# Last norm of a diffusion backbone: most of the mean summed ahead, the gain vector multiplied in earlier, the scaling divided anew

## The chip, the cores and the metric

The kernel runs on one core of one Trainium2 chip. The metric is the device time of one execution in microseconds (us), the median of several runs; lower is better. A core has five engines that run at the same time and wait for each other by semaphores: TensorE (PE, matmuls; PEld is its weight load), VectorE (DVE), ScalarE (ACT), GpSimd (POOL) and SyncE (SP, which only issues DMAs here). ACT and POOL issue DMAs too.

## What is computed

One layer of a backbone for 256 latent and 256 context tokens of width 2048, then a last RMSNorm with its own gain vector. Cut to the end, which the change touches:

```python
def rms_norm(x, g):
    y = x * rsqrt(mean(x * x, axis=-1) + 1e-6)
    return y * g

x = x + gt_a * o_l
h = rms_norm(x, g_ffn) * (1.0 + sc_f) + sh_f
x = x + gt_f * ((silu(h @ wg) * (h @ wu)) @ wd)     # wd: 5632 x 2048
return rms_norm(x, g_final)                         # (1, 256, 2048), float32
```

All of it is float32. Each matmul is made of three with split operands (a high and a low part in the fp32r type).

## The kernel before, in words

Tokens lie on the 128 partitions, in two halves t = 0 and t = 1. Weights are streamed from memory in pieces of 128 x 512 (256 KB); ACT writes the high part (`whi`, L142), DVE the low part (`wlo`, L145), and PE does the three matmuls of each pair (L165, L166, L168). The order of instructions on each engine is the order in which the program writes them down.

The last product (`ffn_wd`) runs in three groups of rows; the last group makes the output columns final. Its blocks of 512 columns are `nb` = 0 to 3. For `nb` 0 to 2, `down_evac` adds the block into the residual `x2` (L1135, L1136), squares it on ACT with a running sum per token into one column of `ss3` (L1137), and multiplies `x2` in place by the gain vector `g_final` (`gfin`, L1139). The in-place multiply must come behind the square, which reads the same columns.

Block `nb` = 3 is done by itself, t = 0 first with 512 columns, then t = 1 in two halves of 256 columns, so that what follows the very last matmul is short (L1156 to L1180). After the matmuls of a part: gate multiply (L1165), residual add (L1166), square with its sum (L1167, which writes its squares over the gate product `yv`). After the last part of a t: the sums in `ss3` are added up (L1169), scaled by 1/2048 with the epsilon added (`rstd_of`, L175), raised to the power -1/2 on POOL (L177). Then the scaling by this factor `r`: block 3 on DVE with the gain vector in the same instruction (L1172), block 0 on DVE (L1176), blocks 1 and 2 on ACT (L1178). Each block then goes to memory with a DMA of 256 KB (L1180): blocks 3 and 1 from SP, blocks 0 and 2 from ACT, in the order 3, 0, 1, 2.

Buffers come from pools that lie one behind the other in SBUF, in the order in which they are opened, one row from the left and one from the right; a name of a pool has as many buffers as the pool says, and each takes a multiple of 32 bytes of a partition. The pool `small` (six buffers for each name) is opened early on the left; behind it come a small pad, the identity, and the streaming pool with `raw`, `whi` and `wlo`, whose first buffer starts at byte 20480 of its partition, then all other pools of the left side (among them `res` with `x2`, `gate` and `tm`, and `ff`). The `y` blocks that the last stores read are in a pool of the right side.

Of the kernel before, what the change touches and what calls it, by code (L numbers as in the profile page):

```python
# [10 lines left out]
F32 = mybir.dt.float32  # L11
F32R = mybir.dt.float32r
AF = mybir.ActivationFunctionType
ALU = mybir.AluOpType
AX = mybir.AxisListType
PSUM = bass.MemoryType.PSUM

P = 128
D = 2048
# [4 lines left out]
EPS = 1e-6  # L24
# [63 lines left out]
def hybrid_dit_kernel(ctx: ExitStack, tc: tile.TileContext, a, out):  # L88
    nc = tc.nc
    pe, act, dve, pool, sp = nc.tensor, nc.scalar, nc.vector, nc.gpsimd, nc.sync  # L90
# [4 lines left out]
    ss3 = const.tile([P, 2, 8], F32, name="ss3")  # L95
    small = ctx.enter_context(tc.tile_pool(name="small", bufs=6))
# [23 lines left out]
    def acc():  # L120
        return psA.tile([P, 512], F32, name="acc")
# [48 lines left out]
    def sub(pair, *sl):  # L170
        return pair[0][sl], pair[1][sl]

    def rstd_of(ssum, n, elems):
        v = small.tile([P, 8], F32, name="ms")
        dve.tensor_scalar(out=v[:, :n], in0=ssum, scalar1=1.0 / elems, scalar2=EPS, op0=ALU.mult, op1=ALU.add)  # L175
        r = small.tile([P, 8], F32, name="rstd")
        pool.tensor_tensor(out=r[:, :n], in0=v[:, :n], in1=mhalf[:, :n], op=ALU.pow)  # L177
        return r

    def tsl(t):  # L180
        return slice(t * P, (t + 1) * P)
# [44 lines left out]
    mhalf = const.tile([P, 8], F32, name="mhalf")  # L226
# [708 lines left out]
    res = ctx.enter_context(tc.tile_pool(name="res", bufs=1))  # L935
    x2 = res.tile([P, 2, D], F32, name="x2")
# [113 lines left out]
    y = [opool.tile([P, 2, 512], F32, name="y", tag="o", bufs=4) for _ in range(4)]  # L1050

    def gu(w, fb):
        accs = [acc() for _ in range(2)]
        for k2 in range(0, KC, 2):
            w_ = stream_w(w, k2, fb * 512, 512)
            mm3s([j for t in range(2) for j in gu_jobs(accs[t], w_, k2, t)])
            side.pump(2.6)
        return accs

    def act_T(sg, ps, pair, t, blocks):  # L1060
        dve.tensor_tensor(out=sg, in0=ps, in1=sg, op=ALU.mult)
        if blocks:


            tr = res.tile([P, 512], F32, name="tm", bufs=2)
            for b in range(4):
                dve.transpose(tr[:, tsl(b)].rearrange("p (j n) -> p j n", j=4), sg.rearrange("p (j b n) -> p b j n", j=4, b=4)[:, b])
            yield 0.0, 1.0
            td = dram.tile([P, 512], F32, name="sgd", bufs=4)
            pool.dma_start(td, tr)  # L1070
            tT = ff.tile([P, 4, 4, 32], F32, name="sg_T", bufs=2)
            dv = td.rearrange("(a p) (b r) -> b p a r", a=4, b=4)
            for b in range(4):
                pool.dma_start(tT[32 * b:32 * b + 32].rearrange("p a j n -> p a (j n)"), dv[b])
            yield 0.0, 14.0
            v = tT.rearrange("p a j n -> p j a n")
            hi, lo = [x[:, :, tsl(t)].rearrange("p j (a n) -> p j a n", a=4) for x in pair]
            act.copy(hi, v)
            dve.tensor_tensor(out=lo, in0=v, in1=hi.bitcast(F32), op=ALU.subtract)
            yield 0.0, 0.0  # L1080
            return
        yield 0.0, 1.5
        transposes_ff(pair, sg, t)
        yield 0.43, 0.0
# [11 lines left out]
    def gate_raw(src, shape):  # L1096
        raw = ff.tile(shape, F32, name="graw", bufs=4)
        pool.dma_start(raw, src)
        return raw

    gate_f = add_ada(5, 6.0, gate_raw, ahead=3)
    for gi, (f0, f1) in enumerate(groups):
        last = gi == len(groups) - 1
        aT, tasks = {}, {}
        for fb in range(f0, f1):
            ga = gu(a["ffn_wg"], fb) if fb else first_g
            sg = []
            for t in range(2):
                s_ = ff.tile([P, 512], F32, name="sg", bufs=4)
                act.activation(s_, ga[t], AF.Silu)  # L1110
                sg.append(s_)
            ua = gu(a["ffn_wu"], fb)
            aT[fb] = (ff.tile([P, 4, S], F32R, name="ah", bufs=6), ff.tile([P, 4, S], F32R, name="al", bufs=6))
            tasks[fb] = [side.add(act_T(sg[t], ua[t], aT[fb], t, fb < f1 - 1), lane="e", width=4) for t in range(2)]
        if gi == 1:
            side.finish(*gate_f)
            gtf = gate_rows(5, res)
            gf = [gate_raw(a["g_final"][i * 1024:(i + 1) * 1024].partition_broadcast(P), [P, 1024]) for i in range(2)]

            def gfin(c):  # L1120
                return gf[c.start // 1024][:, c.start % 1024:c.start % 1024 + c.stop - c.start]

        def down_jobs(ps, w_, fb, j, t):
            return [(ps, sub(aT[fb], slice(None), jj, tsl(t)), w_[jj - j], fb == f0 and jj == 0, fb == f1 - 1 and jj == 3) for jj in (j, j + 1)]

        def down_evac(ps, nb, t):
            c = slice(nb * 512, (nb + 1) * 512)
            if gi == 0:
                act.copy(y[nb][:, t, :], ps)
            elif not last:  # L1130
                dve.tensor_tensor(out=y[nb][:, t, :], in0=ps, in1=y[nb][:, t, :], op=ALU.add)
                dve.tensor_tensor(out=y[nb][:, t, :], in0=y[nb][:, t, :], in1=gtf[:, c], op=ALU.mult)
                dve.tensor_tensor(out=x2[:, t, c], in0=x2[:, t, c], in1=y[nb][:, t, :], op=ALU.add)
            else:
                dve.tensor_tensor(out=y[nb][:, t, :], in0=ps, in1=gtf[:, c], op=ALU.mult)  # L1135
                dve.tensor_tensor(out=x2[:, t, c], in0=x2[:, t, c], in1=y[nb][:, t, :], op=ALU.add)  # L1136
                act.activation(y[nb][:, t, :], x2[:, t, c], AF.Square, accum_out=ss3[:, t, nb:nb + 1])  # L1137
                if nb < 3:
                    dve.tensor_tensor(out=x2[:, t, c], in0=x2[:, t, c], in1=gfin(c), op=ALU.mult)  # L1139

        for nb in range(4 - last):
            accs = [acc() for _ in range(2)]
            for fb in range(f0, f1):
                side.finish(*tasks[fb])
                for j in (0, 2):
                    w_ = stream_w(a["ffn_wd"], fb * 4 + j, nb * 512, 512)
                    mm3s([q for t in range(2) for q in down_jobs(accs[t], w_, fb, j, t)])
                    side.pump(2.6)
            for t in range(2):
                down_evac(accs[t], nb, t)  # L1150
# [5 lines left out]
    for t in range(2):  # L1156
        for c0, cn in (((0, 512),) if t == 0 else ((0, 256), (256, 256))):
            ps = acc()
            for n, (fb, j) in enumerate(steps):
                if t == 0:  # L1160
                    w_keep[fb, j] = stream_w(a["ffn_wd"], fb * 4 + j, 3 * 512, 512, (rt2, 8) if n < 4 else None)
                mm3s([(ps[:, :cn], sub(aT[fb], slice(None), j + kk, tsl(t)), sub(w_keep[fb, j][kk], slice(None), slice(c0, c0 + cn)), n == 0 and kk == 0, n == len(steps) - 1 and kk == 1) for kk in range(2)])
            c = slice(3 * 512 + c0, 3 * 512 + c0 + cn)
            yv = y[3][:, t, c0:c0 + cn]
            dve.tensor_tensor(out=yv, in0=ps[:, :cn], in1=gtf[:, c], op=ALU.mult)  # L1165
            dve.tensor_tensor(out=x2[:, t, c], in0=x2[:, t, c], in1=yv, op=ALU.add)  # L1166
            act.activation(yv, x2[:, t, c], AF.Square, accum_out=ss3[:, t, 3 + (c0 > 0):4 + (c0 > 0)])  # L1167
        ss = small.tile([P, 8], F32, name="ss")
        dve.tensor_reduce(out=ss[:, 0:1], in_=ss3[:, t, :4 + t], axis=AX.X, op=ALU.add)  # L1169
        r = rstd_of(ss[:, 0:1], 1, D)  # L1170
        c = slice(3 * 512, D)
        dve.scalar_tensor_tensor(out=y[3][:, t, :], in0=x2[:, t, c], scalar=r[:, 0:1], in1=gfin(c), op0=ALU.mult, op1=ALU.mult)  # L1172
        for nb in range(3):
            c = slice(nb * 512, (nb + 1) * 512)
            if nb == 0:
                dve.tensor_scalar(out=y[nb][:, t, :], in0=x2[:, t, c], scalar1=r[:, 0:1], scalar2=None, op0=ALU.mult)  # L1176
            else:
                act.activation(y[nb][:, t, :], x2[:, t, c], AF.Copy, scale=r[:, 0:1])  # L1178
        for nb in (3, 0, 1, 2):
            (sp if nb % 2 else act).dma_start(out[tsl(t), nb * 512:(nb + 1) * 512], y[nb][:, t, :])  # L1180
    po.close()


# [59 lines left out]
```

## Time and profile before

| | us |
|---|---|
| median of 3 runs (lowest, highest) | 1357.15 (1356.35, 1359.22) |
| the profiled execution | 1355.29 |
| its span, first to last instruction | 1353.5 |
| PE busy in the span | 1324.0 (98%) |
| DVE busy | 923.2 (68%) |
| ACT busy | 625.7 (46%) |

The profile shows one execution. Start times count from the span's start. A row of the chain of waits gives start, duration and what was running; a row of the timeline gives start, duration, engine, line, operation, output and inputs, and in brackets how long the engine had been idle and what it had waited for. A row of windows gives for a stretch the busy time of each engine with its instructions, the TensorE clock as a share of full speed, the mean busy share of the 16 DMA engines and the rate that they moved. A row of groups gives line, engine, operation, shapes, count, then busy time and the mean nanoseconds of one, then idle time before them.

### The profile page before, as it was taken

To read this page: it belongs to the slowest core of one execution; us is meant where nothing else is said; L and a number is where in the kernel's file an instruction comes from. 1 tells how busy PE (TensorE), PEld (TensorE's weight loads), DVE (VectorE), ACT (ScalarE), POOL (GpSimd) and SP (SyncE) were. 2 spreads that over 40 slices of the span, in tenths; PEclk is the share of its full clock that TensorE was granted. 3 is DMA by queue.
4 is the path that set the end of the run, shared out by engine and by line. 5 is a ranking of instruction groups with operands and counts; after the bars stand their busy time and mean duration, and the time that the engine had idled before them with its cause. 6 is when DMAs were issued, how large, how long until landed. Compare 5 with 4: busy or idle time off the path is not lost.

```text
span 1353.5 us, 21027 instructions
## 1 busy us (share of the span) xinstructions
PE 1324.0 (98%) x7018; PEld 1077.5 (80%) x7018; DVE 923.2 (68%) x1687; ACT 625.7 (46%) x1183; POOL 99.6 (7%) x159
## 2 busy tenths in 40 slices
PE   6999999999999999999999999999999999999997
PEld 4788888778886777777888888888888888888886
DVE  4577789998679747778887954445555566556565
ACT  4532343564334435557445444444444444444453
POOL 1110000100000000000322200001001000011000
PEclk9999999999999999999999999999999999999999
DMA  9999996586687756455999855567667655676553
GB/s 367 344 356 323 322 364 220 171 268 213 198 262 262 247 166 212 135 184 164 344 368 340 307 191 192 193 196 219 210 212 228 218 193 185 203 226 224 193 178 129
DMA packets 190161, 322.29 MB, mean 238 GB/s; under 512 B 22466, under 2 KB 62436, under 8 KB 189028
## 3 DMA queue, kind: packets, MB, share of 16 engines
q1 hardware_dynamic: 177568, 285.28, 63.8%
q0 software_dynamic: 9136, 32.53, 6.5%
q10 hardware_dynamic: 3348, 3.13, 0.7%
q8 instruction: 55, 0.90, 0.3%
q14 instruction: 54, 0.44, 0.1%
HBM read 314.56 MB, written 6.31 MB: 237 GB/s over the span
## 4 chain that ended last, share of the span: by engine, by line
PE 68%; DVE 1%; ACT 1%; DMA 0%; issue 0%; POOL 0%; POOLq 0%; DVEq 0%; SPq 0%; ACTq 0%
PE acc L165 21%; PE acc L168 21%; PE acc L166 21%; PE m L862 1%; PE m L607 1%; PE m L861 1%; PE m L913 1%; PE m L897 1%; PE m L658 1%; DVE wlo L145 0%; PE m L165 0%; PE m L166 0%; PE m L168 0%; ACT whi L142 0%; DMA raw<-in_w_out_dram 0%; PE m L385 0%
## 5 line engine op out<-in xcount | busy, mean ns | idle before, releaser
L145 DVE TENSOR_TENSOR wlo<-raw,whi 128x512 fp32r<-128x512 f32 (+1 forms) x764 | 490.4, 680 | 286.0 <-ACT whi L142 281.5
L142 ACT CAST whi<-raw 128x512 fp32r<-128x512 f32 (+1 forms) x764 | 437.6, 615 | 520.2 <-PE acc L166 427.5
L165 PE MATMUL acc<-whi,h_hi 128*128 128x512 f32 x704 | 274.2, 390 | 0.7 <-ACT h_hi L1013 0.7
L166 PE MATMUL acc<-whi,h_lo 128*128 128x512 f32 x704 | 274.1, 389 | 0.4 <-DVE h_lo L1014 0.4
L168 PE MATMUL acc<-wlo,h_hi 128*128 128x512 f32 x704 | 190.8, 390 | 0.0
L165 PE MATMUL acc<-whi,h 128*128 128x512 f32 (+1 forms) x416 | 161.6, 392 | 1.2 <-ACT tok L791 0.5
L166 PE MATMUL acc<-whi,h 128*128 128x512 f32 (+1 forms) x416 | 157.1, 379 | 0.0
L168 PEld LDWEIGHTS acc<-wlo,h_hi 128*128 128x128 f32 x704 | 132.1, 188 | 28.5 <-DVE wlo L145 1.2
L165 PEld LDWEIGHTS acc<-whi,h_hi 128*128 128x128 f32 x704 | 132.2, 188 | 28.2 <-ACT h_hi L1013 1.1
L166 PEld LDWEIGHTS acc<-whi,h_lo 128*128 128x128 f32 x704 | 132.2, 188 | 28.0 <-DVE h_lo L1014 0.7
L165 PE MATMUL acc<-whi,ah 128*128 128x512 f32 (+1 forms) x364 | 139.1, 384 | 0.0
L166 PE MATMUL acc<-whi,al 128*128 128x512 f32 (+1 forms) x364 | 138.6, 382 | 0.0
L380 DVE SCALAR_TENSOR_TENSOR ada_acc<-raw,cs,ada_acc 128x512 f32<-128x512 f32 x135 | 100.9, 747 | 21.7 <-DMA raw<-in_w_ada_dram 20.2
L168 PE MATMUL acc<-wlo,h 128*128 128x512 f32 (+1 forms) x416 | 114.5, 379 | 1.1 <-DVE wlo L145 1.0
L168 PE MATMUL acc<-wlo,ah 128*128 128x512 f32 (+1 forms) x364 | 96.2, 382 | 0.0
L165 PEld LDWEIGHTS acc<-whi,h 128*128 128x128 f32 x416 | 78.0, 188 | 19.2 <-issue 3.7
L166 PEld LDWEIGHTS acc<-whi,h 128*128 128x128 f32 x416 | 78.2, 188 | 13.4 <-issue 1.2
L168 PEld LDWEIGHTS acc<-wlo,h 128*128 128x128 f32 x416 | 75.9, 188 | 16.2 <-DVE wlo L145 2.5
L165 PEld LDWEIGHTS acc<-whi,ah 128*128 128x128 f32 x364 | 68.4, 188 | 13.3
L166 PEld LDWEIGHTS acc<-whi,al 128*128 128x128 f32 x364 | 68.5, 188 | 13.1
L168 PEld LDWEIGHTS acc<-wlo,ah 128*128 128x128 f32 x364 | 67.6, 188 | 13.3
L177 POOL TENSOR_TENSOR rstd<-ms,mhalf 128x1 f32<-128x1 f32 (+2 forms) x24 | 18.1, 755 | 513.5 <-DVE ms L175 513.5
(238 smaller groups left out, 1419.8 us busy)
## 6 DMA issues: line engine op xcount, KB each, us to landing
raw<-in_ffn_wg_dram SPq DMA_DIRECT2D x176, 256.0 KB, 2.8
raw<-in_ffn_wu_dram SPq DMA_DIRECT2D x176, 256.0 KB, 3.5
raw<-in_ffn_wd_dram SPq DMA_DIRECT2D x176, 256.0 KB, 3.7
raw<-in_w_in_dram SPq DMA_DIRECT2D x144, 256.0 KB, 4.7
raw<-in_w_ada_dram SPq DMA_DIRECT2D x144, 256.0 KB, 3.4
araw<-in_w_ada_dram SPq DMA_DIRECT2D x128, 256.0 KB, 5.1
raw<-in_w_out_dram SPq DMA_DIRECT2D x64, 256.0 KB, 3.4
graw<-in_w_ada_dram POOLq DMA_DIRECT2D x32, 512.0 KB, 6.1
```

Of the source, the lines that this page charges most:

```text
L142: act.copy(hi, raw_)
L145: dve.tensor_tensor(out=lo, in0=raw_, in1=hi.bitcast(F32), op=ALU.subtract)
L165: pe.matmul(dst, lhsT=l[0], rhs=r[0], start=start, stop=False)
L166: pe.matmul(dst, lhsT=l[0 if w_left else 1], rhs=r[1 if w_left else 0], start=False, stop=False)
L168: pe.matmul(dst, lhsT=l[1 if w_left else 0], rhs=r[0 if w_left else 1], start=False, stop=stop)
L177: pool.tensor_tensor(out=r[:, :n], in0=v[:, :n], in1=mhalf[:, :n], op=ALU.pow)
L380: dve.scalar_tensor_tensor(out=acc_, in0=part, scalar=cs[:, 0, kc:kc + 1], in1=acc_, op0=ALU.mult, op1=ALU.add)
L607: pe.transpose(ps[:, tsl(j)], src[:, tsl(j)], ident)
L658: pe.matmul(o[:, :S], lhsT=vt(kc)[:, v0:v0 + P], rhs=pT[:, kc, :], start=(kc == 0), stop=(kc == 3))
L861: pe.matmul(sc, lhsT=ml_qT[:, h, tsl(t)], rhs=ml_kT[:, h, :], start=True, stop=False)
L862: pe.matmul(sc, lhsT=qpeT[hb, h // 2, tsl(t)], rhs=kpeT[hb, :], start=False, stop=True)
L897: pe.matmul(sc, lhsT=df_qT[hb, h, tsl(t)], rhs=df_kT[h // 2][hb, h % 2, :], start=True, stop=True)
```

## The change

Six edits, all in the last group of the last product and the last norm:

1. All squares of this norm take a scale of 1/sqrt(2048), so the sums in `ss3` are already parts of the mean (L1137, L1167).
2. Before the last part of a t is taken from PSUM, DVE sums the columns of `ss3` that are there and adds the epsilon (`part`, a new name in the pool `small`). After the last square only one addition of 128 x 1 is left in front of the power on POOL; L1169 and L175 are gone from there.
3. The square of block 3 writes into a buffer of the existing name `tm` in place of `yv`.
4. DVE multiplies block 3 by the gain vector next to the square, into `yv`; so L1172 becomes a plain scaling.
5. The scaling: DVE takes blocks 3 and 0 and, for t = 1, the first half of block 2; ACT takes the second half of block 2 and block 1. For t = 0 DVE takes block 2 whole.
6. The stores of blocks 3, 0 and 2 are issued from SP, that of block 1 from ACT.

```diff
-                act.activation(y[nb][:, t, :], x2[:, t, c], AF.Square, accum_out=ss3[:, t, nb:nb + 1])
+                act.activation(y[nb][:, t, :], x2[:, t, c], AF.Square, scale=D ** -0.5, accum_out=ss3[:, t, nb:nb + 1])
...
+            end = c0 + cn == 512
+            if end:
+                part = small.tile([P, 1], F32, name="part")
+                dve.tensor_reduce(out=part, in_=ss3[:, t, :3 + t], axis=AX.X, op=ALU.add)
+                dve.tensor_scalar(out=part, in0=part, scalar1=EPS, scalar2=None, op0=ALU.add)
             dve.tensor_tensor(out=yv, in0=ps[:, :cn], in1=gtf[:, c], op=ALU.mult)
             dve.tensor_tensor(out=x2[:, t, c], in0=x2[:, t, c], in1=yv, op=ALU.add)
-            act.activation(yv, x2[:, t, c], AF.Square, accum_out=ss3[:, t, 3 + (c0 > 0):4 + (c0 > 0)])
-        ss = small.tile([P, 8], F32, name="ss")
-        dve.tensor_reduce(out=ss[:, 0:1], in_=ss3[:, t, :4 + t], axis=AX.X, op=ALU.add)
-        r = rstd_of(ss[:, 0:1], 1, D)
-        c = slice(3 * 512, D)
-        dve.scalar_tensor_tensor(out=y[3][:, t, :], in0=x2[:, t, c], scalar=r[:, 0:1], in1=gfin(c), op0=ALU.mult, op1=ALU.mult)
-        for nb in range(3):
-            c = slice(nb * 512, (nb + 1) * 512)
-            if nb == 0:
-                dve.tensor_scalar(out=y[nb][:, t, :], in0=x2[:, t, c], scalar1=r[:, 0:1], scalar2=None, op0=ALU.mult)
+            sq = res.tile([P, 512], F32, name="tm", bufs=2)
+            act.activation(sq[:, :cn], x2[:, t, c], AF.Square, scale=D ** -0.5, accum_out=ss3[:, t, 3 + (c0 > 0):4 + (c0 > 0)])
+            dve.tensor_tensor(out=yv, in0=x2[:, t, c], in1=gfin(c), op=ALU.mult)
+        v = small.tile([P, 8], F32, name="ms")
+        dve.tensor_tensor(out=v[:, 0:1], in0=ss3[:, t, 3 + t:4 + t], in1=part, op=ALU.add)
+        r = small.tile([P, 8], F32, name="rstd")
+        pool.tensor_tensor(out=r[:, 0:1], in0=v[:, 0:1], in1=mhalf[:, 0:1], op=ALU.pow)
+        for nb in (3, 0, 2, 1):
+            src = y[3][:, t, :] if nb == 3 else x2[:, t, nb * 512:(nb + 1) * 512]
+            if nb in (0, 3) or t == 0 and nb == 2:
+                dve.tensor_scalar(out=y[nb][:, t, :], in0=src, scalar1=r[:, 0:1], scalar2=None, op0=ALU.mult)
+            elif nb == 1:
+                act.activation(y[nb][:, t, :], src, AF.Copy, scale=r[:, 0:1])
             else:
-                act.activation(y[nb][:, t, :], x2[:, t, c], AF.Copy, scale=r[:, 0:1])
+                dve.tensor_scalar(out=y[nb][:, t, 0:256], in0=src[:, 0:256], scalar1=r[:, 0:1], scalar2=None, op0=ALU.mult)
+                act.activation(y[nb][:, t, 256:512], src[:, 256:512], AF.Copy, scale=r[:, 0:1])
         for nb in (3, 0, 1, 2):
-            (sp if nb % 2 else act).dma_start(out[tsl(t), nb * 512:(nb + 1) * 512], y[nb][:, t, :])
+            (act if nb == 1 else sp).dma_start(out[tsl(t), nb * 512:(nb + 1) * 512], y[nb][:, t, :])
```

## Rows read from the trace of the kernel before

**Rows 1.** The page: busy time of each engine, and the DMA share in 40 slices.

```profile
PE 1324.0 (98%) x7018; PEld 1077.5 (80%) x7018; DVE 923.2 (68%) x1687; ACT 625.7 (46%) x1183; POOL 99.6 (7%) x159
...
DMA  9999996586687756455999855567667655676553
```

**Rows 2.** The chain that ended last, in order of time (start, duration, what), from 1344 us.

```profile
1344.33 0.25 PE acc L168 x2
...
1344.61 0.44 DVE y L1165
...
1345.07 0.43 DVE x L1166
...
1345.52 0.52 ACT y L1167 x2
...
1346.06 0.17 DVE ss L1169
...
1346.26 0.17 DVE ms L175
...
1346.53 0.58 POOLq L1239
...
1347.14 1.33 ACT y L1178 x2
```

**Rows 3.** The timeline from 1347 us: scalings, and the issues of the last stores.

```profile
1347.14 0.75 DVE L1172 SCALAR_TENSOR_TENSOR y<-x,rstd,graw 128x512 f32<-128x512 f32 x1 [0.73 <-POOL rstd L177]
1347.81 0.48 DVE L1176 TENSOR_SCALAR y<-x,rstd 128x512 f32<-128x512 f32 x1
1347.88 0.81 SPq L1180 DMA_DIRECT2D out_dram<-y  x2
...
1348.31 0.38 SPq L1180 DMA_DIRECT2D out_dram<-y  x1
...
1348.72 0.47 ACTq L1180 DMA_DIRECT2D out_dram<-y  x1
```

**Rows 4.** Windows at the end: engines' busy time, clock, DMA share, GB/s.

```profile
1348.40:1348.70 0.30, 0.00 (x0) 0.00 (x0) 0.00 (x0) 0.07 (x1) 0.00 (x0) 0.50 0.00 0
1348.70:1348.90 0.20, 0.00 (x0) 0.00 (x0) 0.00 (x0) 0.00 (x0) 0.00 (x0) 0.50 0.90 358
...
1349.20:1349.80 0.60, 0.00 (x0) 0.00 (x0) 0.00 (x0) 0.00 (x0) 0.00 (x0) 0.50 1.09 410
...
1351.30:1351.50 0.20, 0.00 (x0) 0.00 (x0) 0.00 (x0) 0.00 (x0) 0.00 (x0) 0.50 0.53 195
...
1351.70:1353.50 1.80, 0.00 (x0) 0.00 (x0) 0.00 (x0) 0.00 (x0) 0.00 (x0) 0.50 0.00 0
```

**Rows 5.** Groups of DVE by shape: a two-input operation of 128 x 1.

```profile
L903 DVE TENSOR_TENSOR l<-st,neglam 128x1 f32<-128x1 f32 x8 | 1.2, 156 | 0.2
```

**Rows 6.** The timeline of ACT: the square of the first half for t = 1.

```profile
1341.46 0.42 ACT L1167 ACTIVATE y<-x 128x256 f32<-128x256 f32 x1 [0.85 <-DVE x L1166]
```

**Rows 7.** The timeline of DVE from 1328 us.

```profile
1332.47 1.31 DVE L1139 TENSOR_TENSOR x<-x,graw 128x512 f32<-128x512 f32 x2 [0.19 <-ACT y L1137]
1335.98 0.69 DVE L1165 TENSOR_TENSOR y<-acc,gate 128x512 f32<-128x512 f32 x1 [2.19 <-PE acc L168]
...
1339.28 0.75 DVE L1172 SCALAR_TENSOR_TENSOR y<-x,rstd,graw 128x512 f32<-128x512 f32 x1 [0.75 <-POOL rstd L177]
...
1340.34 0.42 DVE L1165 TENSOR_TENSOR y<-acc,gate 128x256 f32<-128x256 f32 x1
...
1344.61 0.42 DVE L1165 TENSOR_TENSOR y<-acc,gate 128x256 f32<-128x256 f32 x1 [3.39 <-PE acc L168]
```

**Rows 8.** Groups of ACT by shape, 1250 us to the end: scalings and squares.

```profile
L1178 ACT ACTIVATE y<-x,rstd 128x512 f32<-128x512 f32 x4 | 2.7, 715 | 2.2 <-POOL rstd L177 2.2
...
L1167 ACT ACTIVATE y<-x 128x256 f32<-128x256 f32 x2 | 0.8, 416 | 4.4 <-DVE x L1166 4.4
L1167 ACT ACTIVATE y<-x 128x512 f32<-128x512 f32 x1 | 0.6, 632 | 4.4 <-DVE x L1166 4.4
```

**Rows 9.** Windows of two stretches in which the DMA engines are busy throughout.

```profile
34.00:68.00 34.00, 32.69 (x349) 26.40 (x349) 16.95 (x31) 17.14 (x36) 5.34 (x8) 1.00 1.01 344
...
680.00:714.00 34.00, 34.00 (x154) 28.14 (x153) 32.15 (x54) 18.18 (x32) 8.99 (x13) 1.00 1.01 380
```

## The prediction

> **What bounds the kernel now.** I read the page first. TensorE is busy for 98% of the span [rows 1], so almost all of the time belongs to matmuls, and the change touches none of them. What it can move is the time after the last matmul. The chain that ended last [rows 2] shows it: the last matmul ends at 1344.58, and from there each step waits for the one before it: gate multiply 0.44, residual add 0.43, square 0.52, the sum of the sums 0.17, mean and epsilon 0.17, the power on POOL 0.58, then the scaling from 1347.14. The span ends at 1353.5, so this tail is 8.9 us or 0.66% of the time: that is the whole field.
>
> The chain view stops at the last arithmetic, at 1348.47. The remaining 5.0 us are the stores, for which I read the timeline and the windows. The first store is issued from SP at 1347.88, when the first scaling (0.75) is done, and the fourth from ACT at 1348.72 [rows 3]. The DMA engines are idle until 1348.70 and busy 0.90 of the next 0.2 us, so they begin at about 1348.72, which is 0.84 after the first issue; in the window up to 1351.50 their share is 0.53, so they stop at about 1351.41, and nothing moves in the 2.1 us from there to the end [rows 4]. In between they are full: four stores of 256 KB in 2.69 us, 0.67 each. So the end hangs on the *first* issue plus 0.84 + 2.69 + 2.09, as long as each later store is issued before the engines run dry. All four issues start within 0.84 us while one store takes 0.67 to move, so they do not run dry now.
>
> **The change part by part.** The sum is made against the profiled execution, 1355.29 us (span 1353.5 and 1.79 around it); the median of the runs is 1357.15, 1.86 higher, and I carry the difference in us over to it unchanged.
>
> *The mean summed ahead.* Now two small DVE steps stand between the square and POOL; the step from the start of the first to the start of the second is 0.20 (1346.06 to 1346.26) [rows 2]. In their place stands one addition of 128 x 1; the nearest row is 0.156 [rows 5], as much as one of the two. Gain 0.20. The two operations that make `part` (0.16 and 0.15 by the same kind of row) move in front of the gate multiply of the last part. For t = 1 they need the square of the first half, which ends near 1342.0 [rows 6], and DVE is idle for 3.39 us until 1344.61; for t = 0 it is idle for 2.19 us until 1335.98 [rows 7]. Queued behind them on DVE is only the gate multiply, which waits for PE anyway. Cost nothing; without that idle time it would be 0.31.
>
> *The gain vector beside the square.* A DVE multiply of 256 columns, two inputs, takes 0.43 (as the residual add in [rows 2]), and starts with the square, as both wait for the same residual add. The square and its sum take 0.52, so 0.10 us is left over and it costs nothing. Today the like pair does wait (0.19 on the square, [rows 7]), but there the multiply overwrites what the square reads; here the square gets a buffer of its own so that it doesn't write over `yv`. The first scaling falls from 0.75 to the 0.48 of the plain form [rows 3]: gain 0.27 on the first issue.
>
> *The squares' scale* is a number in an instruction that is there anyway. The trace has no square with another scale than one. A factor per token costs a 512-column ACT operation 0.715 - 0.632 = 0.08 [rows 8], and I take that as the upper end, nothing as the lower, and nothing as my value, since no operand is read.
>
> *Scaling 2.5 to 1.5, stores 3 to 1.* Counted from the moment `r` is there: DVE's second scaling starts 0.08 before the first ends [rows 3], so DVE is done with block 3 at 0.48, block 0 at 0.88 and its half of block 2 at 1.28 at the latest (pricing the half as a whole). ACT's half of block 2 has no row: between 0.416 (256 columns without a factor) and 0.715 (512 with) [rows 8]; I take 0.50, the first plus 0.08. Block 1 is then done between 1.13 and 1.43. SP's issues start 0.43 apart [rows 3]: blocks 3, 0 and 2 at 0.47, 0.90 and 1.33, the block from ACT at 1.43 at the latest. The engines need the second, third and fourth store by 1.14, 1.81 and 2.48. So they never run dry, and the split itself gains nothing at the end.
>
> The stores' queues are the one place where the new form may cost. While SP's queue was alone the rate was 358 GB/s, with both 410 [rows 4]. With three stores on SP about 0.6 us more of the traffic has one queue; at that ratio it would take up to 0.08 longer. The Trainium skill, page "DMA: Bandwidth & Descriptors", section "Issuing engines are not separate DMA queues", says that issuing from several engines saves only issue time, since all run on the same 16 engines; by it this loss is zero. By the rows the sum lies between 0.39 and 0.47. I take the upper value, because the low rate stands at the very start of the traffic, where the share itself is only 0.90.
>
> *t = 0.* Its tail runs beside the matmuls of t = 1. DVE gets three scalings (1.28) in place of 0.75 + 0.40, 0.13 more, against a factor that comes 0.20 sooner, so the first half's gate multiply at 1340.34 [rows 7] is not later. Its stores move before 1344 and meet nothing. Cost nothing; PE does not wait for any of it.
>
> *The sum.* 0.20 + 0.27 = 0.47 us less: 1355.29 becomes 1354.82, and the median 1357.15 becomes **1356.7 us**. Bounds of the unknown costs: 0.31 (both losses) to 0.47.
>
> **The rivals.** A time within 0.2% of the old one, 2.7 us either way, cannot be told from no change; the tail's 8.9 us would have to shrink by almost a third to leave that band.
>
> *The overlap does not happen.* If DVE's multiply waits for the square, the addition is queued behind it on DVE and comes 0.43 later, minus 0.02. Then 0.47 - 0.43 leaves nothing: 1357.1. For it: the like pair waits today [rows 7]. Against: there is no shared buffer left.
>
> *Addresses, the slower side.* `part` is a new name in `small`: six buffers of 32 bytes, 192 bytes, and every pool behind it on the left moves up by that. The streaming buffers start on multiples of 2048 bytes now (20480 is one) and would start 192 bytes past one. Nothing in the trace shows what such a start costs, so the price is bounded by what the DMA engines moved at full share: 344 to 380 GB/s, depending on what was loaded [rows 9], a span of 9.5%. The place is the first six slices, 203 us, in which the engines are busy throughout [rows 1]; elsewhere they have slack behind a full TensorE. From 0 to 19 us, then; no row is nearer to either end, and the middle, 9.6, less 0.47, gives 1366.3. It leaves the band from a loss of 3.2 us, 1.6% of the rate in those slices. Against it: the engines' share of 1.01 beside a full TensorE at 680 us [rows 9] shows that a busy queue need not hold anyone, and each row is still moved as 2 KB. The Trainium skill has a rule for this on the same page, section "How a descriptor splits into AXI transactions": a piece must start on a multiple of 256 bytes, so a start in between costs one part more. By it a row of 2048 bytes at 192 would take 70 beats for 64, an estimate of 9% from that page, which it states for reads; no row here shows it, and the loads write into SBUF.
>
> *The change does more than I see.* If the end followed the last issue instead of the first (1.58 after `r` now, 1.43 at the latest then), the gain would be 0.35 or more: the same band. I have no mechanism for a gain beyond 0.2%; only chance in the runs or a lucky address would give one.
>
> **How the numbers follow.** Forecast 0.70 (1356.7), overlap missing 0.12 (1357.1), addresses 0.14 (1366.3), a lucky gain beyond the band 0.04 (about 1354). So faster 0.04, same 0.82, slower 0.14. The range holds the first two with the spread of the runs, which lie from 0.80 below to 2.07 above their median: 1356.7 - 0.8 = 1355.9, widened to 1355.3 for a part of the lucky cases, and 1357.1 + 2.1 = 1359.2, widened to 1359.9, where the band ends, for the mildest address losses.
>
> **What would show it.** In the changed profile: one DVE operation of 128 x 1 between the last square and POOL; the power on POOL starting about 1.75 us after the last matmul's end, where it is 1.95 now; the multiply by the gain vector beside the square, ended before the square's sum; a plain scaling of 0.48 and the first store issued 0.47 us sooner after the last matmul than now (2.83 instead of 3.30); the DMA engines full for about 2.7 us with no gap; and 2.1 us of silence. The overlap rival would show the multiply's start at the square's end. The address rival would show the last matmul itself later than 1344.6, with a lower rate at full share in the first 200 us. I am wrong if the part up to the last matmul moves by more than the runs' spread, or if the stores' traffic shows a gap.

## The result: slower by 15.6 us, in matmuls that the change does not touch

The changed kernel takes 1372.36 us (median; lowest 1371.91, highest 1376.65) against 1356.75 us for the kernel before, a ratio of 1.0115 with a 95% interval of 1.0099 to 1.013. The profiled execution took 1372.15 us, 16.9 more than that of before. The page of the changed kernel:

```profile
span 1370.4 us, 21035 instructions
...
PE 1338.7 (98%) x7018; PEld 1077.0 (79%) x7018; DVE 926.2 (68%) x1694; ACT 624.1 (46%) x1182; POOL 99.5 (7%) x159
```

TensorE has the same 7018 matmuls as in [rows 1] and is busy 14.7 us longer with them. Its weight loads took as long as before. The chain that ended last shows where the tail now begins (start, duration, what):

```profile
1361.29 0.25 PE acc L168 x2
...
1361.56 0.44 DVE y L1171
...
1362.02 0.43 DVE x L1172
...
1362.48 0.52 ACT tm L1174 x2
...
1363.02 0.17 DVE ms L1177
...
1363.30 0.59 POOLq L1249
...
1363.91 0.49 DVE y L1183
```

The last matmul ends at 1361.54, where it was 1344.58 [rows 2]: 16.96 us later. From there to the end of the span it is 8.86 us, where it was 8.92. So the tail, which is all that the change was about, gained 0.06 us, and the whole loss lies ahead of it.

The matmuls that lost are found in the groups of TensorE. Before (columns as in [rows 5]: count, busy time, mean nanoseconds of one, idle before):

```profile
L165 PE MATMUL acc<-whi,h_hi 128*128 128x512 f32 x704 | 274.2, 390 | 0.7 <-ACT h_hi L1013 0.7
L166 PE MATMUL acc<-whi,h_lo 128*128 128x512 f32 x704 | 274.1, 389 | 0.4 <-DVE h_lo L1014 0.4
L168 PE MATMUL acc<-wlo,h_hi 128*128 128x512 f32 x704 | 190.8, 390 | 0.0
L165 PE MATMUL acc<-whi,ah 128*128 128x512 f32 x340 | 132.8, 391 | 0.0
```

The same groups in the changed kernel:

```profile
L165 PE MATMUL acc<-whi,h_hi 128*128 128x512 f32 x704 | 279.5, 397 | 0.6 <-ACT h_hi L1013 0.6
L166 PE MATMUL acc<-whi,h_lo 128*128 128x512 f32 x704 | 277.7, 395 | 0.4 <-DVE h_lo L1014 0.4
L168 PE MATMUL acc<-wlo,h_hi 128*128 128x512 f32 x704 | 195.3, 396 | 0.1
L165 PE MATMUL acc<-whi,ah 128*128 128x512 f32 x340 | 132.9, 391 | 0.0
```

Three groups became longer, those of the gate and up products, whose weights operand (the one loaded into TensorE ahead of the matmul) is `h_hi` or `h_lo`; the down product with `ah` did not. None waited more: the idle time in front of them is the same within 0.1 us. Matmuls overlap (390 ns each, one every 227 ns), so the better measure is the step from the start of one to the start of the next. The timeline of the weight loads shows it for a dozen matmuls (two weight tiles, two token halves, three products each). Before:

```profile
989.97 0.87 PEld L168 LDWEIGHTS acc<-wlo,h_hi 128*128 128x128 f32 x4
...
992.69 0.87 PEld L168 LDWEIGHTS acc<-wlo,h_hi 128*128 128x128 f32 x4
```

After:

```profile
1000.99 0.89 PEld L168 LDWEIGHTS acc<-wlo,h_hi 128*128 128x128 f32 x4
...
1003.79 0.89 PEld L168 LDWEIGHTS acc<-wlo,h_hi 128*128 128x128 f32 x4
```

A dozen takes 2.80 us instead of 2.72, so a step is 0.2333 instead of 0.2267. There are 3 x 704 such matmuls, 176 dozens: 176 x 0.08 = 14.1 us of the 16.9. The granted clock is 1.00 from 986 to 1020 us in both kernels. The rest lies ahead of them: the first of these matmuls starts at 620.3 us, where it was 617.2.

What do these matmuls have in common? The streamed operand (`whi`, `wlo`), whose columns pass through TensorE, lies in a left pool, which the new name `part` moved up by 192 bytes; `h_hi` and `h_lo` lie in a pool of the right side and stayed. With `ah` and `al`, both operands are on the left and moved together.

### The profile page after: what moved, and what is told of

Its sections match the earlier page's. It is cut to its first block, busy times and chain, and to the rows that moved or that the text cites. A ratio compares the mean times of both kernels' runs of the same rounds, so it can differ in the third digit from the quotient of the medians.

```text
span 1370.4 us, 21035 instructions
## 1 busy us (share of the span) xinstructions
PE 1338.7 (98%) x7018; PEld 1077.0 (79%) x7018; DVE 926.2 (68%) x1694; ACT 624.1 (46%) x1182; POOL 99.5 (7%) x159
## 4 chain that ended last, share of the span: by engine, by line
PE 68%; DVE 1%; ACT 1%; DMA 0%; issue 0%; POOL 0%; POOLq 0%; DVEq 0%; SPq 0%; ACTq 0%
PE acc L165 21%; PE acc L168 21%; PE acc L166 21%; PE m L862 1%; PE m L607 1%; PE m L861 1%; PE m L913 1%; PE m L897 1%; PE m L658 1%; DVE wlo L145 0%; ACT whi L142 0%; PE m L165 0%; PE m L166 0%; PE m L168 0%; PE m L385 0%
## 5 line engine op out<-in xcount | busy, mean ns | idle before, releaser
L165 PE MATMUL acc<-whi,h_hi 128*128 128x512 f32 x704 | 279.5, 397 | 0.6 <-ACT h_hi L1013 0.6
L166 PE MATMUL acc<-whi,h_lo 128*128 128x512 f32 x704 | 277.7, 395 | 0.4 <-DVE h_lo L1014 0.4
L168 PE MATMUL acc<-wlo,h_hi 128*128 128x512 f32 x704 | 195.3, 396 | 0.1
L165 PE MATMUL acc<-whi,o_hi 128*128 128x512 f32 x128 | 51.1, 402 | 1.0 <-ACT whi L142 0.6
```

The lines of the kernel that those rows point to most:

```text
L165: pe.matmul(dst, lhsT=l[0], rhs=r[0], start=start, stop=False)
L166: pe.matmul(dst, lhsT=l[0 if w_left else 1], rhs=r[1 if w_left else 0], start=False, stop=False)
L168: pe.matmul(dst, lhsT=l[1 if w_left else 0], rhs=r[0 if w_left else 1], start=False, stop=stop)
```

## The experiments

The theory after this reading: the step grows when the two operands of a matmul start at different places within 512 bytes, wherever they are. The rivals: the loads into the moved buffers became slower (the prediction's own rival); the streamed operand's own place counts; or the new tail is to blame in some other way.

### The name alone

```diff
+        small.tile([P, 1], F32, name="part")
         ss = small.tile([P, 8], F32, name="ss")
         dve.tensor_reduce(out=ss[:, 0:1], in_=ss3[:, t, :4 + t], axis=AX.X, op=ALU.add)
```

> The kernel before with one line more: a buffer of the new name part in the pool small that nothing uses. Nothing else of the change. It moves every pool behind it on the left side by 192 bytes. If the loss is a matter of addresses (any of three theories: the rows loaded off a boundary, the matmul's streamed operand off a boundary, or the streamed operand and the weights operand of a matmul starting at different places of a 512-byte line), this alone costs what the change cost: about 1372 us, ratio 1.011, and the three matmuls with h_hi and h_lo follow each other every 0.233 us where it was 0.227. If the new tail is the cause (rival), it stays at 1357.

1372.38 us, ratio 1.0107 (1.0089 to 1.0125). A buffer that nothing reads or writes costs the whole loss. Its group of the gate and up products:

```profile
L165 PE MATMUL acc<-whi,h_hi 128*128 128x512 f32 x704 | 279.7, 397 | 0.7 <-ACT h_hi L1013 0.7
```

### The change without the name

```diff
-                part = small.tile([P, 1], F32, name="part")
+                part = small.tile([P, 8], F32, name="ss")[:, 0:1]
```

> The whole change, but part is taken as a column of a buffer of the existing name ss, so that no pool moves. Address theories: the loss is gone and what is left is the tail, 1356.3 to 1356.8 us (the prediction's 0.47 less at most), ratio 0.9995 to 1.000, the last matmul at the old 1344.6 us. Rival, the new tail is the cause: 1372 us.

1356.43 us, ratio 0.9996 (0.9986 to 1.0006). The loss is gone with the name, and the rest of the change cannot be told from nothing by time. The two runs together settle it: the shift of addresses is the cause, the new tail is not.

### Both sides moved, and the right side alone

```diff
-    edge.tile([P, 120], F32, name="edge_pad")
+    edge.tile([P, 72], F32, name="edge_pad")
```

with the unused name (both sides move up by 192 bytes):

> The kernel before with the unused name part and with the right side's pad made 192 bytes smaller, so that the right side's pools move up by the same 192 bytes as the left side's. Theory that the difference between the two operands of a matmul counts: back to about 1357 us and 0.227 us for the matmuls with h_hi and h_lo. Rival, loads that write rows 192 bytes past a boundary: still about 1372. Rival, the streamed operand's own place counts: still about 1372.

and without it (the right side alone):

> The kernel before with the right side's pad 192 bytes smaller and no new name: the streamed weights stay where they were, h_hi and h_lo move by 192 bytes. Theory that the difference between the operands counts: about 1372 us, with 0.233 us for the matmuls with h_hi and h_lo. Rivals (loaded rows, or the streamed operand's own place): about 1357, since neither the stream's buffers nor their loads move.

1363.74 us (1.0048, 1.003 to 1.0065) and 1364.17 us (1.0051, 1.0031 to 1.0071). Neither theory had half of the loss, so the times alone decide nothing; the groups do. Both sides moved:

```profile
L165 PE MATMUL acc<-whi,h_hi 128*128 128x512 f32 x704 | 274.2, 390 | 0.7 <-ACT h_hi L1013 0.7
L166 PE MATMUL acc<-whi,h_lo 128*128 128x512 f32 x704 | 274.1, 389 | 0.4 <-DVE h_lo L1014 0.4
L168 PE MATMUL acc<-wlo,h_hi 128*128 128x512 f32 x704 | 191.0, 390 | 0.2
```

The right side alone:

```profile
L165 PE MATMUL acc<-whi,h_hi 128*128 128x512 f32 x704 | 276.0, 392 | 0.7 <-ACT h_hi L1013 0.7
```

With both moved, these matmuls are as fast as before, although both operands start 192 bytes past the old place: it is the difference that counts, not either place. With the right side alone moved, they lose again, but less, and the difference now has the other sign. (The expectation for this run was the full loss, 0.233; a dozen takes 2.75 us here, 0.229 a step.) What the first of these kernels loses lies elsewhere, ahead of these matmuls, the first of which starts at 625.4 us for 617.2. Its windows (columns as in [rows 9]):

```profile
34.00:68.00 34.00, 30.19 (x323) 23.59 (x322) 15.52 (x29) 18.51 (x39) 1.92 (x4) 0.95 1.03 335
68.00:102.00 34.00, 33.73 (x306) 27.78 (x306) 24.73 (x51) 10.68 (x19) 6.60 (x6) 0.95 0.97 318
```

and a shorter one inside the first two:

```profile
66.00:70.00 4.00, 4.00 (x18) 3.81 (x18) 1.24 (x3) 0.14 (x1) 3.37 (x7) 0.50 0.91 250
```

Before, these stretches moved 344 [rows 9] and 354 GB/s at a granted clock of 1.00 of TensorE's full 2.4 GHz; here it is 335, then 318, and TensorE does fewer matmuls (323 for 349, 306 for 355). It stood idle for 3.05 us until 65.67, and from about 65 to 72 us its clock was at the lower level (0.50 in the last row). With the right side alone moved the first stretch moved 335 GB/s, too. Moving the right side moves the buffers of the first loads, so these two runs mix two effects, which the next ones keep apart; that the slower loads led to the idle time and the lower clock is likely, but no run shows it by itself.

### Only `h_hi` and `h_lo` moved

An unused buffer of the wanted size behind these two in their own pool moves them down, with the small pool of the second norm beside them; no buffer that is loaded from memory moves.

```diff
+    h2p.tile([P, 80], F32, name="h2_pad")
     tp = p_tp.enter_context(tc.tile_pool(name="tp", bufs=1, side="right"))
```

First in the changed kernel, with 320 bytes, so that both operands again start alike within 512:

> The change as it is, with an unused buffer of 320 bytes behind h_hi and h_lo in their pool: only these, and the small pool of the second norm next to them, move, by 320 bytes downwards, so that both operands of the gate and up matmuls start 192 bytes past a multiple of 512. No load moves. Theory that the difference between the two operands costs TensorE time: these matmuls are back at 0.227 us from one to the next, the 14.3 us that they lost are back, and about 1358 us remain (1.5 above the kernel before, from stages ahead of them). Rival, the rows loaded off a boundary: still 1372.

1360.37 us, ratio 1.0021 (1.0011 to 1.003). The group is back at 390 ns:

```profile
L165 PE MATMUL acc<-whi,h_hi 128*128 128x512 f32 x704 | 274.2, 390 | 0.7 <-ACT h_hi L1014 0.7
```

So 12 of the 15.6 us are given back by a pad that touches nothing of the change, and some 3 us stay (2.9 by the ratio, 3.6 by the medians). Then in the kernel before, where the stream keeps its place and only the difference is new:

> The kernel before with an unused buffer of 192 bytes behind h_hi and h_lo: only these move, 192 bytes down, and the streamed weights start 192 bytes further from them (the same difference as in the change). Theory of the difference: 0.2335 us from one matmul with h_hi or h_lo to the next, +14.3 us, about 1371. Rival, loads off a boundary: 1357, since no load's place changes.

1370.68 us (ratio 1.0099, 1.0078 to 1.0119): nearly the whole loss without moving one load. The rival that prices the loads cannot give this. Its group:

```profile
L165 PE MATMUL acc<-whi,h_hi 128*128 128x512 f32 x704 | 279.7, 397 | 0.7 <-ACT h_hi L1014 0.7
```

Other distances, each with one run:

> The same with 320 bytes, which is 192 the other way round within 512. If the difference counts within 512 bytes and has a direction, it is what the run with the right side alone moved showed: 0.229 us, about +4.6 us. If only its size counts, 0.2335 and +14.3.

> The same with 256 bytes. If the pattern repeats every 256 bytes or less, as before: 0.227 us and 1357. If it repeats every 512: some loss between the two neighbours, 0.229 to 0.2335.

> The kernel before with an unused buffer of 128 bytes behind h_hi and h_lo. Differences of 0 and 256 bytes cost nothing, 192 costs 0.0066 us a matmul, 320 (64 beyond 256) costs 0.0022. If the cost grows with the difference up to the period: 0.229 to 0.2335 between matmuls, some 1361 to 1371 us.

> The same with 32 bytes, the smallest step of the pools. If the cost grows with the difference: half of that of 64 bytes or so, 0.228 us between matmuls, about 1359 us. If any difference off the period costs alike in steps of 64: 0.227 or 0.229.

A dozen matmuls, as above, for 320, 256, 128 and 32 bytes, in this order, each from its own kernel:

```profile
991.69 0.87 PEld L168 LDWEIGHTS acc<-wlo,h_hi 128*128 128x128 f32 x4
...
994.44 0.88 PEld L168 LDWEIGHTS acc<-wlo,h_hi 128*128 128x128 f32 x4
```

```profile
991.24 0.87 PEld L168 LDWEIGHTS acc<-wlo,h_hi 128*128 128x128 f32 x4
...
993.96 0.87 PEld L168 LDWEIGHTS acc<-wlo,h_hi 128*128 128x128 f32 x4
```

```profile
992.59 0.89 PEld L168 LDWEIGHTS acc<-wlo,h_hi 128*128 128x128 f32 x4
...
995.38 0.88 PEld L168 LDWEIGHTS acc<-wlo,h_hi 128*128 128x128 f32 x4
```

```profile
990.87 0.89 PEld L168 LDWEIGHTS acc<-wlo,h_hi 128*128 128x128 f32 x4
...
993.67 0.89 PEld L168 LDWEIGHTS acc<-wlo,h_hi 128*128 128x128 f32 x4
```

| `h_hi`, `h_lo` moved down by | a dozen, us | time, us | against 1356.7 |
|---|---|---|---|
| 32 bytes | 2.80 | 1370.41 | +13.7 |
| 128 bytes | 2.79 | 1368.55 | +11.9 |
| 192 bytes | 2.80 | 1370.68 | +14.0 |
| 256 bytes | 2.72 | 1356.53 | -0.2 |
| 320 bytes | 2.75 | 1361.68 | +5.0 |

A difference of 256 bytes costs nothing, 32, 128 and 192 cost nearly the same, 320 costs a third, as the right side alone did, whose difference is 320 within 512, too. If the pattern repeats every 256 bytes, 320 stands for 64; 64 itself was not tried. My guess that the cost grows with the difference is wrong: 32 costs more than 128 and much more than 320.

### The left side moved by 256 in all

```diff
-    pad.tile([P, 8], F32, name="left_pad")
+    pad.tile([P, 24], F32, name="left_pad")
```

in the changed kernel, `part` and all:

> The change as it is, with the left side's pad 64 bytes larger: with the 192 bytes of part the left side's pools move up by 256 in all. Theory that the operands' difference counts with a period of 256 bytes, and that the rest of the loss (3.4 us in the run with the change and h_hi, h_lo moved) comes from loads that start off a multiple of 256: both are gone, 1356.4 us, ratio 0.9996, as with the change without the new name. If the rest has to do with another boundary (512 and up), about 1360 with 0.227 us between the matmuls. If any move of the left side costs, 1372.

1356.9 us, ratio 0.9998 (0.9989 to 1.0008). The whole loss is gone, the 3 us of the run with `h_hi` and `h_lo` moved as well. A part of those can be seen in the stretch in which loads fill the DMA engines. With `h_hi` and `h_lo` moved and the left side 192 bytes up:

```profile
646.00:680.00 34.00, 34.00 (x152) 28.15 (x151) 30.36 (x53) 15.05 (x26) 12.49 (x20) 1.00 1.00 354
680.00:714.00 34.00, 33.90 (x151) 27.51 (x150) 29.28 (x47) 17.16 (x30) 9.96 (x14) 1.00 1.02 358
714.00:748.00 34.00, 33.84 (x151) 27.50 (x150) 25.44 (x46) 17.45 (x31) 7.87 (x14) 1.00 1.01 339
```

With the left side 256 up:

```profile
646.00:680.00 34.00, 34.00 (x152) 28.16 (x151) 30.57 (x53) 14.64 (x26) 12.29 (x20) 1.00 0.99 358
680.00:714.00 34.00, 34.00 (x154) 28.14 (x153) 30.43 (x48) 17.91 (x31) 10.11 (x14) 1.00 1.01 368
714.00:748.00 34.00, 34.00 (x153) 27.90 (x152) 25.28 (x47) 17.32 (x31) 7.66 (x13) 1.00 0.94 327
```

Divided by the share, the first moved 354, 351 and 336 GB/s, the second 362, 364 and 348: 2 to 4% less in each stretch. Other kernels agree in the second and third stretch: with the stream 192 bytes up (the change, the name alone, both sides moved) 341 to 348 and 338 to 341 GB/s, with it in its old place (before, the right side alone, `h_hi` and `h_lo` 192 down) 366 to 376 and 349 to 353; in the first stretch the two sorts overlap. The first kernel above stayed full into the third stretch, and TensorE lost a few matmuls. From the first gate matmul to the first down matmul it took 180.6 us against 179.3. These 1.3 us are also all that the two profiled executions differ by (1358.27 and 1356.95 us); the first is a quick one, its median is 1360.37, and what the longer executions lose besides stays open. Ahead of 617 us the profiles tell nothing on it, since kernels that are alike there differ by up to 2.1 us in the start of the first gate matmul. The Trainium skill, page "DMA: Bandwidth & Descriptors", section "How a descriptor splits into AXI transactions", says that pieces start on multiples of 256 bytes; that 256 is harmless and 192 is not fits it, but no run moved the loads alone, and the 9% that was worked out from it is not what is seen.

### The stores two and two

The change without the name, with the old division of the stores:

```diff
-            (act if nb == 1 else sp).dma_start(out[tsl(t), nb * 512:(nb + 1) * 512], y[nb][:, t, :])
+            (sp if nb % 2 else act).dma_start(out[tsl(t), nb * 512:(nb + 1) * 512], y[nb][:, t, :])
```

> The change without the new name, and the stores issued as before, blocks 3 and 1 from SP, 0 and 2 from ACT. It looks at the tail alone, in the profile: with three stores on SP the four stores took 2.85 us to move where they took 2.69, and the end came 0.06 us sooner after the last matmul, not 0.47. If the one queue is the cause: 2.7 us again and an end 8.5 to 8.6 us after the last matmul. If it is not: 2.85 and 8.8 to 8.9.

1357.01 us in one run, which says nothing on 0.3 us; its profile does. The last matmul ends at 1346.61 and the span at 1355.2, 8.6 us, where three stores on SP have 8.86 in the change and 8.8 in the change without the name. The chain and the issues (timeline) of this kernel:

```profile
1346.36 0.25 PE acc L168 x2
```

```profile
1347.56 0.42 DVE L1175 TENSOR_TENSOR y<-x,graw 128x256 f32<-128x256 f32 x1
...
1349.55 0.96 SPq L1190 DMA_DIRECT2D out_dram<-y  x2
...
1349.95 0.85 ACTq L1190 DMA_DIRECT2D out_dram<-y  x2
```

The first store is issued 2.94 us after the last matmul, 0.06 later than in the change, and yet the end comes 0.27 us sooner. The scatter is much smaller: from the last matmul to the end it is 8.90 to 8.92 us in all nine kernels with the old tail, and 8.84 to 8.87 in all four with three stores on SP. So the three-to-one division takes back most of what the tail gains. The run does not tell what in the division does it: with two and two the last store comes from ACT, with three to one from SP.

Windows at its end:

```profile
1350.30:1350.50 0.20, 0.00 (x0) 0.00 (x0) 0.00 (x0) 0.00 (x0) 0.00 (x0) 0.50 0.54 215
...
1352.80:1353.00 0.20, 0.00 (x0) 0.00 (x0) 0.00 (x0) 0.00 (x0) 0.00 (x0) 0.50 0.93 307
1353.00:1355.20 2.20, 0.00 (x0) 0.00 (x0) 0.00 (x0) 0.00 (x0) 0.00 (x0) 0.50 0.09 32
```

Read as in the prediction, the DMA engines begin at about 1350.39 and are busy for 2.79 us, which leaves 2.0 us to the end.

## Why the prediction was wrong

**What bounds the kernel: half right.** The tail is 0.66% of the time and the change shortened it by 0.06 us. But the sentence that the change touches no matmul was wrong. It touched their operands' addresses, and 2112 of the 7018 matmuls follow each other 3% more slowly (0.2333 us for 0.2267), which is 14.1 us.

**The address rival: right in the place of origin, wrong in the mechanism and in the chance.** It named `part`, the 192 bytes and the last matmul as the sign to look for, and gave 1366.3 us at a chance of 0.14. It sought the cost in the loads of the first 203 us. The lower rate that it named as a sign there did not show: from 34 to 102 us the changed kernel moved 342 and 358 GB/s, where it was 344 and 354. The runs put about 14 us into matmuls from 617 us on, which the run with only `h_hi` and `h_lo` moved gives alone; about 3 us remain when these are set right (the run of the change with `h_hi` and `h_lo` moved), and the loads are only their likely cause. The step that failed is "elsewhere they have slack behind a full TensorE": it took a full TensorE for one that cannot be slowed. TensorE's own rate was the thing that fell. The argument against the rival, that a full queue need not hold anyone and a row is still 2 KB, spoke only of loads. That 1366.3 is nearer to the measured 1372.36 than the forecast is luck: its price came from loads, and the loss did not. Since two of the kernel's own buffers are unused pads that bring the pools' starts onto multiples of 512, the code did show that such starts exist and can be set; the prediction looked only at the left side's starts and asked only who loads into the pools, not which instruction reads from both sides at once.

**The mean summed ahead: right.** One operation of 0.17 stands where two stood; the power starts 1.76 us after the last matmul's end (1363.30), as forecast (1.75), instead of 1.95.

**The gain vector beside the square: right.** In the timeline of the changed kernel it starts with the square and ends 0.1 us ahead of the square's sum, and the first scaling takes 0.49. The overlap rival is out. The issues:

```profile
1362.48 0.42 DVE L1175 TENSOR_TENSOR y<-x,graw 128x256 f32<-128x256 f32 x1
...
1364.42 1.31 SPq L1190 DMA_DIRECT2D out_dram<-y  x3
...
1365.06 0.35 ACTq L1190 DMA_DIRECT2D out_dram<-y  x1
```

The first store is issued 2.88 us after the last matmul, 0.42 sooner than before (3.30, [rows 2, 3]), against 0.47 forecast. Of the missing 0.05, 0.04 lie between the start of the first scaling and that issue: 0.51 us, where 0.47 was taken.

**The stores three to one: mis-sized.** The prediction gave them a loss of 0 to 0.08 and took 0. Windows at the end of the changed kernel:

```profile
1365.20:1365.40 0.20, 0.00 (x0) 0.00 (x0) 0.00 (x0) 0.00 (x0) 0.00 (x0) 0.50 0.64 256
...
1368.00:1368.20 0.20, 0.00 (x0) 0.00 (x0) 0.00 (x0) 0.00 (x0) 0.00 (x0) 0.50 0.44 164
1368.20:1370.40 2.20, 0.00 (x0) 0.00 (x0) 0.00 (x0) 0.00 (x0) 0.00 (x0) 0.50 0.01 5
```

The engines start at about 1365.27 (0.85 after the first issue, as before) and stop at about 1368.09: 2.82 us for the four stores, where [rows 4] give 2.69; then 2.3 us to the end, where it was 2.1. So the sum "first issue + 0.84 + 2.69 + 2.09" held in its first two terms alone, and the two others took back 0.35 of the 0.42. With the stores divided two and two, 0.33 us of the tail is gained. Of the two terms, the division acts through the last: in that run, too, the engines are busy for 2.79 us, but from there to the end it is 2.0 us and not 2.3. The prediction held that term fixed at 2.09 and looked for a loss only in the rate. Why the end comes later behind the traffic is not shown. The Trainium skill, page "DMA: Bandwidth & Descriptors", section "Issuing engines are not separate DMA queues", says that issuing from several engines saves only issue time. For the traffic the trace agrees (2.79 and 2.82 us); but all issues were early enough, and the end still moved by 0.27 us.

**The range** ended at 1359.9, where the address losses began, so the likeliest of the bad cases was cut off whole.

## What to carry to other kernels

A new buffer name is an edit to every address behind it. Before an edit is judged by its own cost, ask which pools it moves, and keep starts where they were: reuse an existing name, as the change without `part` does (1356.43 us), or pad to a multiple of 256 bytes (1356.9, no loss left). When a matmul-bound kernel slows with no new wait, compare the step between matmuls by operand group; the group that changed names the operands.

## What the runs showed of the hardware that was not expected

- The step between fp32r matmuls of 512 columns depends on where their two operands start relative to each other in SBUF: 0.2267 us at a difference of 0 or 256 bytes, 0.2333 at 192 and at 32, 0.2325 at 128 and 0.229 at 320 (the kernel: 1370.68, 1370.41, 1368.55 and 1361.68 us for 1356.7). Either operand may be moved; moving both alike costs these matmuls nothing (390 ns in the groups). Why, and what the steps in between look like, stays open: six differences were tried, and only with weights of 128 columns.
- Not every matmul is touched. The transposes multiply the identity, which lies on the left and moved by 192 bytes, with tiles of the right side that stayed (`p` and `tok`, float32, 128 columns): one most often follows the other after 0.109 us in the kernel before and in the changed one (mean of a group 275 ns and 274 ns in both).
- Loads into buffers that start 192 bytes past a multiple of 256 moved some 3% less at a full share than with 256 (351 against 364 GB/s in one stretch). The loads were not moved alone.
- Four stores of 256 KB ended 0.27 us later with three of them on SP than with two and two, though the first was issued 0.06 us sooner; the traffic took as long (2.82 and 2.79 us), the time behind it did not (2.3 and 2.0).
